# A decoder layer whose feed-forward part gets a written-out order on every engine

## The chip, the cores and the metric

The kernel runs on one core of a Trainium2 chip. The core has five engines that work side by side, each with its own queue of instructions that it takes in order: TensorE (PE: matrix products and transposes; PEld is its loading of the stationary operand), VectorE (DVE), ScalarE (ACT), GpSimd (POOL) and SyncE (SP, which here only issues DMAs). They meet through semaphores. The metric is the time of one execution on the device in microseconds.

## The reference, cut to what matters

One step of a one-layer decoder, for a prompt of 1024 rows and 8 sample rows with the same weights; the model width is 1024, the feed-forward width 22 x 128 = 2816. The change lies behind the mixing of the two attention paths:

```python
mixed = (jax.nn.sigmoid(ga) * y_att + jax.nn.sigmoid(gb) * y_ret) @ w_o
x = _layer_norm(DEEPNORM_ALPHA * x + gate1 * mixed, ln1_g, ln1_b)
h2 = x * (1 + scale2) + shift2
f_gate, f_up = jnp.split(h2 @ w_ffn_in, 2, axis=-1)
ff = (jax.nn.silu(f_gate) * f_up) @ w_ffn_out
x = _layer_norm(DEEPNORM_ALPHA * x + gate2 * ff, ln2_g, ln2_b)
```

gate, scale and shift are vectors computed from c at the start. Beside this the outputs hold the rolled key and value caches of the sample rows, which are copied by DMAs of some 2 MB through the whole kernel.

## The kernel before, in words

**Products.** Each f32 operand is split in two parts: ScalarE casts the raw tile to `hi` (L158), VectorE subtracts to get `lo` (L159). A product is three matmuls: hi x hi, hi x lo, lo x hi (`mm3`, L195 to L197; `product`, L1033 to L1036).

**w_o and the first layer norm.** Four chunks of 256 columns of the transposed activations (the first also has the 8 sample rows). In each, 8 blocks `f` of 24 matmuls; ScalarE evacuates a block into `gm` with the gate (L1084). After the 8 blocks `norm_block` runs for each 128 rows: 8 transposes of gm into `ps_a` (L939), residual and layer norm on VectorE, 8 transposes of x into `ps_b` (L949), and h2. After two chunks `combine_chunk` forms the seven left operands X1 to X7 of a half.

**First matrix of the feed-forward.** A 2 x 2 scheme with seven products. A job is one block of 128 columns of the gate and of the up part. `pair_load` loads the two weight tiles g and u and has GpSimd form four sums of them (L1006 to L1009); `pair_split` splits the four tiles that result (two products each from the first three, one from the last); `pair_steps` runs the seven steps, each of 12 matmuls for one half of the rows, with the evacuations by ScalarE (copies L1044, L1052, L1058; SiLU L1049, L1068) and VectorE (L1048, L1059, L1063, L1064, L1067, L1069) into the tile `c`. The result goes to DRAM (`ffd`, L1070). There are 25 jobs: 3 with half 1 alone, 19 with both halves (168 matmuls each), 3 with half 0 alone. While jobs run, `roll` starts one cache copy per split: VectorE copies one element (`tk`, L171), GpSimd copies it on (`tick`, L172) and issues the DMA (L174).

**Second matrix.** For half 1, then half 0: 8 column blocks `f`, each 22 x 3 matmuls into each of two banks, with the weights in three groups of 8, 8 and 6 row blocks. The activations come back from DRAM (`ffr`, L1110) and are split into `xk`. ScalarE evacuates into `z` (L1221); after every second f, z is transposed for each block of 128 rows (L1236), VectorE adds it to y (L1237) and takes statistics (L1238). GpSimd scales and shifts the residual (L1193). `finish` does the last layer norm: for half 1 on GpSimd (L1160, L1167) with the write of y on SP's queue (L1168), for half 0 on VectorE (L1162, L1172).

**What sets the order.** The program is written as loops, and a scheduler of the language orders the instructions of each engine by its own estimates: an instruction may be put ahead of others that stand before it in the text as long as its data allow. Tiles come from rings (`stream`, by tag) and from a list of free slots; an instruction that writes a tile waits until its former readers are done. On the chip an engine keeps the order that it was given.

## Time and profile before

| | us |
|---|---|
| median of 3 runs | 1992.9 (1992.45 to 1998.88) |
| profiled execution | 1996.48 |
| its span | 1994.7 |
| mean granted TensorE clock in it | 0.965 |
| TensorE busy | 1859.9 (93%) |
| VectorE, ScalarE, GpSimd busy | 966.3, 678.5, 474.5 |

The profile shows one execution. Its stages from w_o on, by the first matmul of each: w_o at 1020.4 us, first single jobs at 1143.9, jobs with both halves from about 1200 to 1640, last single jobs to 1686, second matrix to 1977.2, then the last layer norm and the writes to 1994.7. A clock of 1.00 is the full 2.4 GHz, the lower level is half of that; a mean between them says how much of a stretch ran at which.

### The profile page before, as it was taken

The page shows a single profiled execution, that of the slowest core. Times are in us where ns is not written, and L with a number is a line of the kernel's source. Part 1 is how long each engine was busy: PE and PEld are TensorE (multiplying, and loading weights), DVE is VectorE, ACT ScalarE, POOL GpSimd, SP SyncE. Part 2 cuts the span into 40 slices and gives each one's busy share as a digit, 9 for nine tenths or more (in the row PEclk, how much of TensorE's full clock was granted, in tenths as well). Part 3 has the DMA queues.
Part 4 walks back from the last instruction along what each step waited for, and adds up shares of the span by engine and source line. Part 5 has one row for each costly group of instructions (what it writes and reads, how often), then busy time and mean ns, then how long its engine had stood idle before and what let it go on. Part 6 is the DMA issues. An engine that isn't in the chain of part 4 may idle for free. (4 is left out here: it accounts for less than half of the span.)

```text
span 1994.7 us, 33810 instructions
## 1 busy us (share of the span) xinstructions
PE 1859.9 (93%) x13974; PEld 1760.4 (88%) x13974; DVE 966.3 (48%) x2009; ACT 678.5 (34%) x1327; POOL 474.5 (24%) x492
## 2 busy tenths in 40 slices
PE   7999999999999999999998879999999997899796
PEld 5979798899989999999998778989899887899696
DVE  4644546676443422214549583345444558435324
ACT  3251424343433421223236543333332344224221
POOL 2000010320000000000024445433432446504800
PEclk9999999999999999999999889999999998999898
DMA  9212131852231344512145534344554557435331
GB/s 289 74 36 92 33 110 54 221 178 75 67 102 53 112 146 146 156 54 64 54 148 190 161 129 135 136 149 149 192 204 144 192 169 226 137 97 177 119 93 59
DMA packets 263899, 255.34 MB, mean 128 GB/s; under 512 B 9701, under 2 KB 243533, under 8 KB 262978
## 3 DMA queue, kind: packets, MB, share of 16 engines
q1 hardware_dynamic: 240530, 138.48, 23.9%
q0 software_dynamic: 23088, 114.61, 16.7%
q8 instruction: 109, 1.79, 0.4%
q14 instruction: 44, 0.36, 0.1%
q10 hardware_dynamic: 128, 0.10, 0.0%
HBM read 222.25 MB, written 74.94 MB: 149 GB/s over the span
## 5 line engine op out<-in xcount | busy, mean ns | idle before, releaser
L159 DVE TENSOR_TENSOR w_lo<-w_raw,w_hi 128x1024 fp32r<-128x1024 f32 (+1 forms) x186 | 235.3, 1266 | 398.9 <-ACT w_hi L158 397.3
L158 ACT CAST w_hi<-w_raw 128x1024 fp32r<-128x1024 f32 (+1 forms) x202 | 203.0, 1005 | 433.3 <-PE ps_d L196 223.3
L195 PE MATMUL ps_d<-h_hi,w_hi 128*128 128x384 f32 (+1 forms) x1008 | 325.5, 323 | 0.0
L197 PE MATMUL ps_d<-h_hi,w_lo 128*128 128x384 f32 (+1 forms) x1008 | 323.7, 321 | 0.0
L196 PE MATMUL ps_d<-h_lo,w_hi 128*128 128x384 f32 (+1 forms) x1008 | 323.2, 321 | 0.0
L1216 PE MATMUL ps_d<-xk,w_hi 128*128 128x260 f32 (+1 forms) x704 | 201.2, 286 | 1.2 <-DVE xk L159 1.2
L1215 PE MATMUL ps_d<-xk,w_hi 128*128 128x260 f32 (+1 forms) x704 | 201.5, 286 | 0.0
L1217 PE MATMUL ps_d<-xk,w_lo 128*128 128x260 f32 (+1 forms) x704 | 200.4, 285 | 0.0
L1033 PE MATMUL ps_b<-X,w_hi 128*128 128x260 f32 (+1 forms) x528 | 160.6, 305 | 38.7 <-ACT w_hi L158 29.5
L195 PEld LDWEIGHTS ps_d<-h_hi,w_hi 128*128 128x128 f32 x1008 | 189.5, 188 | 5.2 <-DVE A L846 3.3
L197 PEld LDWEIGHTS ps_d<-h_hi,w_lo 128*128 128x128 f32 x1008 | 189.7, 188 | 1.7 <-issue 1.2
L196 PEld LDWEIGHTS ps_d<-h_lo,w_hi 128*128 128x128 f32 x1008 | 189.7, 188 | 0.8 <-issue 0.4
L1036 PE MATMUL ps_b<-X,w_lo 128*128 128x260 f32 (+1 forms) x528 | 158.9, 306 | 2.7 <-DVE w_lo L159 1.7
L1035 PE MATMUL ps_b<-X,w_hi 128*128 128x260 f32 (+1 forms) x528 | 158.7, 301 | 0.0
L1033 PEld LDWEIGHTS ps_b<-X,w_hi 128*128 128x128 f32 x528 | 109.7, 208 | 43.3 <-ACT w_hi L158 32.5
L1216 PEld LDWEIGHTS ps_d<-xk,w_hi 128*128 128x128 f32 x704 | 134.9, 192 | 1.4 <-DVE xk L159 1.4
L1215 PEld LDWEIGHTS ps_d<-xk,w_hi 128*128 128x128 f32 x704 | 135.0, 192 | 0.1
L1217 PEld LDWEIGHTS ps_d<-xk,w_lo 128*128 128x128 f32 x704 | 135.1, 192 | 0.0
L172 POOL COPY tick<-tk 1x1 f32<-1x1 f32 x54 | 39.6, 734 | 385.3 <-DVE tk L171 374.0
L363 PE MATMUL ps_d<-w_lo,h_hi 128*128 128x256 f32 x448 | 127.3, 285 | 0.7 <-DVE w_lo L159 0.7
L361 PE MATMUL ps_d<-w_hi,h_hi 128*128 128x256 f32 x448 | 127.5, 285 | 0.0
L362 PE MATMUL ps_d<-w_hi,h_lo 128*128 128x256 f32 x448 | 126.7, 283 | 0.0
(358 smaller groups left out, 4605.1 us busy)
## 6 DMA issues: line engine op xcount, KB each, us to landing
w_raw<-w_in SPq DMA_DIRECT2D x56, 512.0 KB, 4.5
w_raw<-w_ffn_in SPq DMA_DIRECT2D x50, 512.0 KB, 4.0
ada_raw<-w_ada SPq DMA_DIRECT2D x32, 512.0 KB, 4.9
w_raw<-w_o SPq DMA_DIRECT2D x32, 512.0 KB, 3.9
w_raw<-w_ffn_out SPq DMA_DIRECT2D x32, 512.0 KB, 3.9
sample_k<-cache_k POOLq DMA_DIRECT2D x8, 2047.0 KB, 9.4
sample_v<-cache_v POOLq DMA_DIRECT2D x8, 2047.0 KB, 9.3
ada_raw<-w_ada SPq DMA_DIRECT2D x32, 256.0 KB, 5.3
```

Source lines behind the costliest of these rows:

```text
L158: nc.scalar.copy(hi, raw)
L159: eng.tensor_sub(lo, raw, hi.bitcast(F32))
L195: nc.tensor.matmul(ps, whi[:, k0 + k, :], xhi[:, t0:t0 + n], start=f, stop=False)
L196: nc.tensor.matmul(ps, whi[:, k0 + k, :], xlo[:, t0:t0 + n], start=False, stop=False)
L197: nc.tensor.matmul(ps, wlo[:, k0 + k, :], xhi[:, t0:t0 + n], start=False, stop=l)
L361: nc.tensor.matmul(ps[:, j, :], xh, whi, start=k == 0, stop=False)
L1033: nc.tensor.matmul(ps, whi[:, w, :], xhi[:, k, :n], start=first and k == 0, stop=False, skip_group_check=True)
L1035: nc.tensor.matmul(ps, whi[:, w, :], xlo[:, k, :n], start=False, stop=False, skip_group_check=True)
L1036: nc.tensor.matmul(ps, wlo[:, w, :], xhi[:, k, :n], start=False, stop=k == 3, skip_group_check=True)
L1215: nc.tensor.matmul(ps, whi[:, kk, :], xt[:, 0, j, :n], start=st_, stop=False)
L1216: nc.tensor.matmul(ps, whi[:, kk, :], xt[:, 1, j, :n], start=False, stop=False)
L1217: nc.tensor.matmul(ps, wlo[:, kk, :], xt[:, 0, j, :n], start=False, stop=en)
```

## The change

Everything up to w_o is as before. From there on TensorE, VectorE, ScalarE, GpSimd and SP are reached through a wrapper, `InOrder`, which pins each traced instruction behind the one that was traced before it on the same engine, so the text's order is the engine's order. A few calls still go past the wrapper (w_o's loads and splits, the layer norm's VectorE work). The text is rewritten to suit:

- `norm_block` is a generator in two parts. The first part of a block (transposes of gm, residual, norm) runs after one of the next chunk's w_o blocks, the second (transposes of x, h2) some blocks later; those of the last chunk run between the products of the first single jobs.
- In a job both halves' products of a step are issued first, then both evacuations. The splits stand at fixed steps: tile 2 and 3 of the running job after steps 0 and 1, tile 0 and 1 of the next job after steps 2 and 4. The four sums of the next job follow step 0, the loads of the one after it step 1. u is loaded into a slot, g into the ring. Cache copies start in the jobs with both halves, four a job instead of three, and in half 1 of the second matrix.
- In the second matrix the weights are loaded four groups ahead and split two ahead. The transposes of a pair of f come after the first group of the next f, the blocks in a row. The activations' loads are on SP's queue, half 1's writes of y on GpSimd's, and the residual's scale and shift on VectorE. The last f of half 0 is done bank by bank, with the norm of two blocks after each.

The core of the diff:

```diff
+class InOrder:
+    def __init__(self, tc, eng):
+        self.tc, self.eng = tc, eng
+
+    def __getattr__(self, op):
+        f = getattr(self.eng, op)
+
+        def call(*args, **kw):
+            return self.tc.keep_in_program_order(f(*args, **kw))
+
+        return call
...
+    def psplit(raw, hi, lo):
+        act.copy(hi, raw)
+        dve.tensor_sub(lo, raw, hi.bitcast(F32))
...
         layer_norm(x, rows)
         dma_o.dma_start(xr[tb:tb + rows], x[:rows])
+        yield
         for half in range(2):
             pb = bbank((128, 4, rows))
             for j in range(4):
                 f = 4 * half + j
-                nc.tensor.transpose(pb[:, j, :], x[:rows, 128 * f:128 * f + 128], ident[:rows, :rows])
+                pe.transpose(pb[:, j, :], x[:rows, 128 * f:128 * f + 128], ident[:rows, :rows])
...
+    def norm_chunk(ci, gm):
+        t0 = QCH[ci][0]
+        todo = [(t0, 128), (t0 + 128, 128)] + ([(S, NB)] if ci == 3 else [])
+        gens = []
+        for tb, rows in todo:
+            dst = h2s
+            if tb < S:
+                dst = H2[tb // 128] = slots.alloc((128, 8, 128), name="h2")
+            g_ = norm_block(tb, rows, gm, t0, dst)
+            next(g_)
+            gens.append(g_)
+            yield
+        slots.free(*gm)
+        if ci == 0:
+            combine_chunk(1)
+            yield
+        for g_ in gens:
+            next(g_)
+            yield
+
...
+    def pair_sums(q):
+        if q >= NJ:
+            return
+        g, _, u, _ = raws[q]
         s_, e = slots.alloc((128, 8, 128), name="w_s"), slots.alloc((128, 4, 128), name="w_s4")
...
-        nc.scalar.copy(c11, pa)
+        yield
+        act.copy(c11, pa)
         yield
         pg = dbank((128, n))
         product(pg, q, 0, 1, x[2], n, True)
-        nc.vector.tensor_add(c11, c11, pg)
-        nc.scalar.activation(c11, c11, AF.Silu)
...
-    JOBS = [(i, (1,)) for i in range(LEAD)] + [(i, (1, 0)) for i in range(LEAD, FFC)] + [(i, (0,)) for i in range(LEAD)]
+    pending = deque()
+
+    def step_pending():
+        while pending:
+            try:
+                next(pending[0])
+                return
+            except StopIteration:
+                pending.popleft()
+
+    def after_chunk(ci, gm):
+        yield from norm_chunk(ci, gm)
+        if ci % 2 == 0:
+            if ci == 2:
+                combine_chunk(3)
+            combine_chunk(ci)
+            yield
...
         for f in range(8):
             ps = dbank((128, n))
             o0 = t0 % 512
-            mm3(ps, wo_cols(f), [(m[ci // 2][:, 0, :], m[ci // 2][:, 1, :]) for m in mix], o0, n)
+            whi, wlo = wo_cols(f)
+            for k, m in enumerate(mix):
+                xhi, xlo = m[ci // 2][:, 0, o0:o0 + n], m[ci // 2][:, 1, o0:o0 + n]
+                pe.matmul(ps, whi[:, k, :], xhi, start=k == 0, stop=False)
+                pe.matmul(ps, whi[:, k, :], xlo, start=False, stop=False)
+                pe.matmul(ps, wlo[:, k, :], xhi, start=False, stop=k == 7)
             dst = gm[f // 2][:, f % 2, :]
             nc.scalar.activation(dst[:, :256], ps[:, :256], AF.Copy, scale=modT[:, GATE1 + f, 8:9])
             if n > 256:
                 nc.vector.tensor_mul(dst[:, 256:n], ps[:, 256:n], modT[:, GATE1 + f, 0:NB])
+            step_pending()
         if ci % 2 == 0:
             slots.free(*[m[ci // 2] for m in mix])
...
-        dma_o.dma_start(raw[:, :, :n], ffd[k, half].rearrange("p (a b) -> p a b", a=2)[:, :, :n])
+        sp.dma_start(raw[:, :, :n], ffd[k, half].rearrange("p (a b) -> p a b", a=2)[:, :, :n])
         t = xk[half][k] = slots.alloc((128, 2, 2, 260), F32R, name="xk")
-        split(raw[:, :, :n], t[:, 0, :, :n], t[:, 1, :, :n])
+        return raw, t, n
...
     for q, (i, halves) in enumerate(JOBS):
...
         steps = [pair_steps(q, i, half) for half in halves]
         for s_ in range(7):
-            for g_ in steps:
-                next(g_)
-            if more and s_ in (1, 3, 5):
-                pair_split(q + 1, s_ // 2)
-            if q >= FFC and 1 <= s_ < 5:
-                ff_load(1, ORDER[4 * (q - FFC) + s_ - 1])
...
+            for _ in range(2):
+                for g_ in steps:
+                    next(g_)
+            if s_ == 0:
+                pair_split(q, 2)
+                pair_sums(q + 1)
+            elif s_ == 1:
+                pair_split(q, 3)
+                pair_load(q + 2)
+            elif s_ == 2:
+                pair_split(q + 1, 0)
+            elif s_ == 4:
+                pair_split(q + 1, 1)
+            if len(halves) == 1 and s_ % 2 == 0 or q > LEAD - 2:
+                step_pending()
...
+            pool.tensor_mul(y[:rows], y[:rows], ln2[0][:rows])
+            pool.tensor_add(y[:rows], y[:rows], ln2[1][:rows])
+            pool.dma_start(dst, y[:rows])
...
+    def residual(e):
+        y, rows = e[0], e[3]
+        dve.scalar_tensor_tensor(y[:rows], y[:rows], ALPHA, ln1[0][:rows], op0=OP.mult, op1=OP.mult)
+        dve.scalar_tensor_tensor(y[:rows], ln1[1][:rows], ALPHA, y[:rows], op0=OP.mult, op1=OP.add)
...
+        out_mm(G, (0, 1))
...
+        if G > 0:
+            out_split(G + 2)
+        out_load(G + 4)
+        if o0 == 0 and later:
+            for e in ents[later[0]]:
+                add_block(e, *later[1:])
+            slots.free(later[2])
+            if later[:2] == (1, 7):
+                late_ys = deque(ents[1])
+            later = None
...
-        finish(*e)
+                later = (half, f, z)
```

In the rows below a number behind a name only tells tiles apart, and in the kernel after all instructions that the wrapper passes have the wrapper's line, L116.

**ScalarE, around the start of a job with both halves.** `c4` are the output tiles of the two halves, `ps_b` a bank of products, `w_s` and `w4` tiles of sums. Before:

```order
L1044 COPY c4_367_12206<-ps_b_12207 128x260
L1044 COPY c4_368_12221<-ps_b_12222 128x256
L1049 ACTIVATE c4_367_12206<-c4_367_12206 128x260
L1049 ACTIVATE c4_368_12221<-c4_368_12221 128x256
L158 CAST w_hi_12131<-w_s_360_12061 128x1024
L158 CAST w_hi_12168<-w_raw_12058 128x1024
L158 CAST w4_hi_363_12192<-w_s4_361_12062 128x512
L158 CAST w_hi_12266<-w_raw_12196 128x1024
L1052 COPY c4_367_12206<-ps_b_12207 128x260
L1052 COPY c4_368_12221<-ps_b_12222 128x256
L1058 COPY c4_367_12206<-ps_b_12207 128x260
L1058 COPY c4_368_12221<-ps_b_12222 128x256
```

and now:

```order
L116 COPY c4_371_12396<-ps_b_12397 128x260
L116 COPY c4_372_12410<-ps_b_12411 128x256
L116 CAST w_hi_12426<-w_raw2_364_12071 128x1024
L116 ACTIVATE c4_371_12396<-c4_371_12396 128x260
L116 ACTIVATE c4_372_12410<-c4_372_12410 128x256
L116 CAST w4_375_12470<-w_s4_368_12192 128x512
L116 COPY c4_371_12396<-ps_b_12397 128x260
L116 COPY c4_372_12410<-ps_b_12411 128x256
L116 CAST w_hi_12507<-w_raw_12234 128x1024
L116 COPY c4_371_12396<-ps_b_12397 128x260
L116 COPY c4_372_12410<-ps_b_12411 128x256
L116 CAST w_hi_12569<-w_s_373_12434 128x1024
```

Before, the job's remaining casts stand in a row behind the SiLUs of its second step; now each cast stands alone between evacuations, and the last one belongs to the next job already.

**TensorE, at the end of the first w_o chunk.** `ps_d_10440` is that chunk's last block, `gm` its evacuated blocks, `mix` the activations. Before:

```order
L196 MATMUL ps_d_10440<-mix_283_10063,w_hi_10443 128x264
L197 MATMUL ps_d_10440<-mix_283_10063,w_lo_10444 128x264
L939 MATMUL ps_a_10476<-ident_72,gm_285_10205 128x128 x2
L939 MATMUL ps_a_10476<-ident_72,gm_286_10206 128x128 x2
L939 MATMUL ps_a_10482<-ident_72,gm_287_10207 128x128 x2
L939 MATMUL ps_a_10482<-ident_72,gm_288_10208 128x128
L195 MATMUL ps_d_10601<-mix_269_9167,w_hi_10604 128x256
L196 MATMUL ps_d_10601<-mix_269_9167,w_hi_10604 128x256
```

and now, where `ps_d_10477` is the next chunk's first block, which follows ps_d_10440:

```order
L116 MATMUL ps_d_10477<-mix_281_9935,w_lo_10481 128x256
L116 MATMUL ps_d_10477<-mix_283_10063,w_hi_10480 128x256 x2
L116 MATMUL ps_d_10477<-mix_283_10063,w_lo_10481 128x256
L116 MATMUL ps_a_10512<-ident_72,gm_285_10205 128x128 x2
L116 MATMUL ps_a_10512<-ident_72,gm_286_10206 128x128 x2
L116 MATMUL ps_a_10518<-ident_72,gm_287_10207 128x128 x2
L116 MATMUL ps_a_10518<-ident_72,gm_288_10208 128x128 x2
L116 MATMUL ps_d_10534<-mix_269_9167,w_hi_10537 128x256 x2
```

Before, the transposes of gm follow the chunk's last block at once; now the next chunk's whole first block is between.

**SP's queue in half 0 of the second matrix.** `w_raw` are the weights' tiles, `y` the finished rows of half 1. Before:

```order
L1208 DMA w_raw_18979<-w_ffn_out 128x8x128
L1208 DMA w_raw_19033<-w_ffn_out 128x8x128
L1168 DMA y_prompt<-y_538_17120 128x1024
L1168 DMA y_prompt<-y_539_17121 128x1024
L1208 DMA w_raw_19087<-w_ffn_out 128x3x128 x2
L1168 DMA y_prompt<-y_540_17122 128x1024
L1168 DMA y_prompt<-y_541_17123 128x1024
L1208 DMA w_raw_19135<-w_ffn_out 128x8x128
L1168 DMA y_sample<-y_542_17124 8x1024
L1208 DMA w_raw_19189<-w_ffn_out 128x8x128
```

and now:

```order
L116 DMA w_raw_18768<-w_ffn_out 128x8x128
L116 DMA w_raw_18838<-w_ffn_out 128x8x128
L116 DMA w_raw_18896<-w_ffn_out 128x3x128 x2
L116 DMA w_raw_18954<-w_ffn_out 128x8x128
L116 DMA w_raw_19013<-w_ffn_out 128x8x128
L116 DMA w_raw_19087<-w_ffn_out 128x3x128 x2
```

The writes of y have left this queue (they stand on GpSimd's); only loads of weights follow each other here.

## Rows read from the trace of the kernel before

**Rows 1.** Windows: per stretch busy time of each engine (x instructions), PEclk, DMA share, GB/s.
```profile
1020.40:1143.90 123.50, 110.13 (x886) 108.08 (x886) 83.42 (x147) 67.36 (x121) 52.06 (x31) 0.96 0.60 189
1143.90:1200.00 56.10, 43.91 (x307) 41.33 (x308) 46.29 (x76) 26.66 (x51) 24.19 (x29) 0.85 0.40 130
1274.44:1298.39 23.95, 21.98 (x170) 21.51 (x169) 9.37 (x19) 7.28 (x14) 10.32 (x12) 0.93 0.38 132
1322.39:1342.34 19.95, 19.95 (x170) 19.95 (x169) 6.38 (x14) 4.88 (x11) 5.79 (x7) 1.00 0.48 159
1640.00:1686.00 46.00, 33.66 (x230) 32.65 (x230) 37.53 (x44) 22.71 (x40) 29.20 (x33) 0.82 0.75 241
1686.00:1977.20 291.20, 266.41 (x2178) 263.74 (x2177) 109.24 (x170) 80.44 (x115) 97.89 (x61) 0.95 0.38 116
1900.00:1950.00 50.00, 50.00 (x423) 49.56 (x422) 15.88 (x25) 11.34 (x15) 0.00 (x0) 1.00 0.32 93
1977.20:1994.70 17.50, 1.56 (x10) 0.82 (x8) 13.73 (x28) 1.43 (x5) 0.00 (x0) 0.68 0.32 120
```

**Rows 2.** Waits of TensorE, 1018 us to the end: us in total, times, longest.
```profile
PE ps_b L1033 <- ACT w_hi L158: 29.5, 15, 2.0
PE ps_a L1236 <- ACT z L1221: 23.6, 5, 14.7
PE ps_a L939 <- ACT gm L1084: 12.2, 5, 4.2
...
PE ps_d L1216 <- DVE xk L159: 1.2, 1, 1.2
```

**Rows 3.** Timeline between two jobs: start, us, engine, operation [idle before].
```profile
1439.19 0.42 ACT L1049 ACTIVATE c<-c 128x256 f32<-128x256 f32 x1 [0.99 <-DVE c L1048]
1439.51 1.03 ACT L158 CAST w_hi<-w_s 128x1024 fp32r<-128x1024 f32 x1
...
1440.45 1.04 ACT L158 CAST w_hi<-w_raw 128x1024 fp32r<-128x1024 f32 x1
...
1440.59 0.48 PE L1033 MATMUL ps_b<-X,w_hi 128*128 128x260 f32 x1 [1.96 <-ACT w_hi L158]
```

**Rows 4.** Groups by line, jobs with both halves: x count, busy, mean ns, idle before.
```profile
L159 DVE TENSOR_TENSOR w_lo<-w_raw,w_hi 128x1024 fp32r<-128x1024 f32 x39 | 51.7, 1326 | 2.3 <-ACT w_hi L158 2.1
...
L172 POOL COPY tick<-tk 1x1 f32<-1x1 f32 x31 | 32.6, 1053 | 88.1 <-DVE tk L171 76.8 <-DVE c L1067 11.2
```

**Rows 5.** Timeline of VectorE and GpSimd in a last single job.
```profile
1642.95 4.95 DVE L159 TENSOR_TENSOR w_lo<-w_raw,w_hi 128x1024 fp32r<-128x1024 f32 x1
1642.99 1.38 POOL L1007 TENSOR_TENSOR w_s<-w_s,w_raw 128x512 f32<-128x512 f32 x1
...
1645.43 1.37 POOL L1009 TENSOR_TENSOR w_s<-w_raw,w_s 128x512 f32<-128x512 f32 x1
```

**Rows 6.** Timeline of ScalarE at a chunk boundary of w_o.
```profile
1076.44 1.04 ACT L158 CAST w_hi<-w_raw 128x1024 fp32r<-128x1024 f32 x1
1077.39 0.47 ACT L1084 ACTIVATE gm<-ps_d,modT 128x256 f32<-128x256 f32 x1
```

**Rows 7.** Timeline in half 0 of the second matrix.
```profile
1868.82 4.64 POOL L1167 TENSOR_TENSOR y<-y,ln_b 128x1024 f32<-128x1024 f32 x2
1871.18 2.65 SPq L1168 DMA_DIRECT2D y_prompt<-y  x2
...
1877.91 0.83 ACT L158 CAST w_hi<-w_raw 128x768 fp32r<-128x768 f32 x1 [16.41 <-DMA w_raw<-w_ffn_out]
```

**Rows 8.** Timeline of VectorE behind transposes of half 1.
```profile
1726.71 0.41 DVE L1237 TENSOR_TENSOR y<-y,ps_a 128x256 f32<-128x256 f32 x1
...
1727.98 0.42 DVE L1238 BATCH_NORM_STATS2 bny<-y 128x6 f32<-128x256 f32 x1
```

**Rows 9.** Timeline of VectorE in the tail.
```profile
1980.92 1.28 DVE L1162 SCALAR_TENSOR_TENSOR y<-y,bnmv,ln_g 128x1024 f32<-128x1024 f32 x1
...
1983.44 2.73 DVE L1172 SCALAR_TENSOR_TENSOR y<-y,bnr,ln_b 128x512 f32<-128x512 f32 x4
```

More of the change, by code (lines that the diff above doesn't have):

```diff
@@ L1113, in ff_load, with out_load @@
         slots.free(raw)
-    rolling[0] = True
+    GROUPS = [(half, f, o0, nk) for half in (1, 0) for f in range(8) for o0, nk in ((0, 8), (8, 8), (16, 6))]
+    NG = len(GROUPS)
+    graw, gw = {}, {}
+    def out_load(G):
+        if G >= NG:
+            return
+        _, f, o0, nk = GROUPS[G]
+        raw = graw[G] = stream.tile([128, nk, 128], F32, tag="raw", name="w_raw")
+        ks = ORDER[o0:o0 + nk]
+        k1 = next((j for j in range(1, nk) if ks[j] != ks[j - 1] + 1), nk)
+        for j0, j1 in ((0, k1), (k1, nk)):
+            if j1 > j0:
+                sp.dma_start(raw[:, j0:j1, :], w_fo[128 * ks[j0]:128 * (ks[j0] + j1 - j0), 128 * f:128 * f + 128]
+                             .rearrange("(k p) c -> p k c", p=128))
@@ L1116, in tile_hybrid_decoder_step, with out_split @@
+    def out_split(G):
+        if G >= NG:
+            return
+        nk = GROUPS[G][3]
+        hi = stream.tile([128, nk, 128], F32R, tag="hi", name="w_hi")
+        lo = stream.tile([128, nk, 128], F32R, tag="lo", name="w_lo")
+        psplit(graw.pop(G)[:], hi[:], lo[:])
+        if rolling[0]:
+            roll(hi)
+        gw[G] = (hi, lo)
+    waiting = deque()
+    kq = 0
     for q, (i, halves) in enumerate(JOBS):
-        more = q + 1 < len(JOBS)
+        rolling[0] = len(halves) == 2
@@ L1136, in tile_hybrid_decoder_step, with bcast @@
+    assert not pending
     free_x(X[0])
[L1137 to L1140 removed]
+    def bcast(names):
         ts = []
@@ new lines, in add_block @@
+    def add_block(e, f, z):
+        y, st, tb, rows, _, _ = e
+        c = slice(128 * (f - 1), 128 * f + 128)
+        pz = abank((rows, 256))
+        for p in range(2):
+            if tb < S:
+                b = tb // 128 % 4
+                src = z[:, p, b % 2, 128 * (b // 2):128 * (b // 2) + 128]
+            else:
+                src = zs[:, f - 1 + p, :]
+            pe.transpose(pz[:, 128 * p:128 * p + 128], src, ident[:])
+        dve.tensor_add(y[:rows, c], y[:rows, c], pz)
+        dve.bn_stats(st[:rows, f // 2, :], y[:rows, c])
@@ new lines, in tile_hybrid_decoder_step, with out_mm @@
+    zs = late.tile([128, 8, NB], F32, name="zs")
+    ln1, ln2 = bcast(("ln1_g", "ln1_b")), bcast(("ln2_g", "ln2_b"))
+    ents = {1: list(load_ys(1))}
+    todo = deque(ents[1])
+    later = None
+    late_ys = deque()
+    pss = None
+    rolling[0] = True
+    def out_mm(G, js):
+        half, f, o0, nk = GROUPS[G]
+        n = HALF[half]
+        whi, wlo = gw[G]
+        for j in js:
+            for kk in range(nk):
+                xt = xk[half][ORDER[o0 + kk]]
+                pe.matmul(pss[j], whi[:, kk, :], xt[:, 0, j, :n], start=o0 + kk == 0, stop=False)
+                pe.matmul(pss[j], whi[:, kk, :], xt[:, 1, j, :n], start=False, stop=False)
+                pe.matmul(pss[j], wlo[:, kk, :], xt[:, 0, j, :n], start=False, stop=o0 + kk == FFC - 1)
@@ new lines, in evac, with refill, drain @@
+    def evac(half, f, z, j):
+        act.activation(z[:, f % 2, j, :256], pss[j][:, :256], AF.Copy, scale=modT[:, GATE2 + f, 8:9])
+        if half:
+            dve.tensor_mul(zs[:, f, 4 * j:4 * j + 4], pss[j][:, 256:260], modT[:, GATE2 + f, 4 * j:4 * j + 4])
+    def refill(half, room):
+        k = len(xk[half])
+        if k < FFC and len(slots.free_list) >= room:
+            waiting.append(ff_load(half, ORDER[k]))
+            return True
+    def drain():
+        while waiting:
+            ff_split(waiting.popleft())
@@ new lines, in tile_hybrid_decoder_step @@
+        out_mm(G, (0, 1))
+        if half and f == 7:
+            for k in ORDER[o0:o0 + nk]:
+                slots.free(xk[1][k])
+        rolling[0] = bool(half)
+        if G > 0:
[7 more added lines that the diff above has]
+                late_ys = deque(ents[1])
+            later = None
+        if o0 == 16:
+            for j in range(2):
+                evac(half, f, z, j)
+            if f % 2:
+                later = (half, f, z)
@@ new lines, in tile_hybrid_decoder_step @@
+        if half and f == 6 and o0 == 16:
+            while refill(0, 5):
+                pass
+            drain()
+        if half and f == 7:
+            for _ in range(nk):
+                refill(0, 5)
+                if len(waiting) > 2:
+                    ff_split(waiting.popleft())
+            drain()
+        if not half and f == 0:
+            while refill(0, 2):
+                pass
+            drain()
+            if o0 == 16:
+                ents[0] = list(load_ys(0))
+                todo = deque(ents[0])
@@ L1250 @@
+        if todo and o0 < 16:
+            residual(todo.popleft())
+            if todo:
+                residual(todo.popleft())
+        if late_ys and o0 == 8:
+            finish(*late_ys.popleft())
+    assert not copies, len(copies)
 OUTPUTS = ([("y_prompt", (S, D)), ("y_sample", (NB, D))]
```

253 lines of the change are left out of this document (111 added, 142 removed).

## The prediction

> **What bounds the kernel now.** I read the windows by stage first, then what TensorE waited for, then the timeline at those waits. All rows are from the stretch that the change touches, 1020 us to the end; nothing ahead of it is edited, so I cost that part at nothing.
>
> The windows give the price of a matmul at the full clock: 423 instructions in 50 us with no idle time, 118 ns each [rows 1]. With it each stage's own work is worked out from its count in the window, and the rest of the stage is loss: w_o 886 x 0.118 = 104.5 of 123.5 us, 19.0 lost; the first single jobs 307 x 0.118 = 36.2 of 56.1, 19.9 lost; the last single jobs 230 x 0.118 = 27.1 of 46.0, 18.9 lost; the second matrix 2184 (2112 matmuls and 72 transposes by the loops) x 0.118 = 257.7 of 291.2, 33.5 lost; the tail 17.5 with TensorE nearly still [rows 1].
>
> For the 19 jobs with both halves, compare two of them: one takes 23.95 us at a clock of 0.93, another 19.95 us at 1.00 [rows 1]. 19.95 is 168 x 0.118 = 19.8, so the second loses nothing. The list of waits shows why the other is longer: TensorE waits for w_hi 15 times, 29.5 us in all, longest 2.0 [rows 2]; the four others of the 19 don't. So a stalled job loses 2.0 us of waiting and another 2.0 to matmuls that run at the lower of the two clocks behind it (the mean of 0.93 against 1.00) and to small waits for w_lo. The timeline of one shows the mechanism: on ScalarE the SiLU of the second half (1439.19) ends, only then the cast of w_hi starts (1439.51), and TensorE, idle for 1.96 us, starts in 1440.59 [rows 3]. The cast needed nothing that was late; its data were loaded and summed. It stood behind the SiLU, which stood behind VectorE's addition, which stood behind the last matmul of the second product. 15 x 4.0 = 60 us is the largest sum that the profile offers.
>
> **The change, part by part.** *Jobs with both halves.* The order of ScalarE now puts each cast ahead of the SiLU or behind a copy, at least one step ahead of need. A step is 24 matmuls, 24 x 0.118 = 2.83 us. Step 0's copies end about 0.4 us after it, at 3.2; the cast for steps 4 and 5 takes 1.04 [rows 3], to 4.3; VectorE's w_lo 1.33 [rows 4], to 5.6; needed at 4 x 2.83 = 11.3. The next job's first cast follows step 2's copies, 8.9, done with its w_lo at 11.3, needed at 19.8; its second follows step 4's copies, 14.5, done at 16.9, needed at 25.5. The slack is 5.7 us or more each time. What can use it up is GpSimd: its four sums follow step 0 too, and they hold VectorE up. One w_lo took 4.95 us while three sums of 1.37 to 1.38 ran [rows 5], 3.6 more than the mean of 1.33. With all four ahead of it, 4 x 1.37 = 5.5, w_lo ends at 11.1 against 11.3: just in time. Ends for this part: all 60 us gone, or the present loss kept (0). I take 55, since the middle case is in time by rows and a few jobs will miss.
>
> The Trainium skill (SBUF — State Buffer, Who interferes with whom) states that a VectorE instruction with two SBUF inputs and a GpSimd instruction that reads SBUF exclude each other, and that the one that issues first keeps the port for its whole instruction. By that alone w_lo would wait for one sum; here it outlasted three, so the trace is harsher than the rule read instruction by instruction. By the rule this part would give 60; by the row it gives the rival with a kept wait, below.
>
> *w_o and the layer norms.* Before, the transposes of gm stand right behind the last block of a chunk, whose evacuation has to come first; TensorE waits for gm 5 times, 12.2 us, longest 4.2 [rows 2]. Now a whole block of 24 matmuls (2.83 us) lies between. But the evacuation still stands on ScalarE behind a cast of the next w_o block: 1.04 and 0.47 [rows 6], and that cast needs a buffer which the running block lets go. So I expect 1.5 to 2 us to stay at each of three chunk boundaries, and the clock to fall there again. Between 0 and 15 of the 19.0; I take 6, half of the waiting on gm.
>
> *First single jobs.* The last chunk's norms, the combinations and their splits now come between the products. VectorE is busy 46.3 of 56.1 us there [rows 1] and loses none of this work, so at best 9.8 come back; and with a pinned order an instruction of VectorE that waits for a transpose holds up the w_lo behind it. From 4 lost to 9.8 gained: I take 2 gained.
>
> *Last single jobs.* VectorE 37.5 of 46.0 us, clock 0.82 [rows 1]: at best 8.5 come back, by loading and splitting the activations of the second matrix one at a time between steps. Here a late ffr holds up ScalarE's queue, as nothing may pass it. Ends 5 lost and 8.5 gained; I take 5 gained.
>
> *Second matrix.* Of its 33.5 us, 23.6 are waits of the transposes for z [rows 2]. The longest, 14.7: ScalarE stood 16.41 us in a cast that waited for its w_raw [rows 7]; the load stood on SP's queue behind the writes of y_prompt, and those behind GpSimd's normalisation of y, 2.3 us an instruction (4.64 for two) [rows 7]. Now SP holds loads alone there, the writes are on GpSimd's queue, where only GpSimd waits for them, and the residual left GpSimd for VectorE, which has room (15.9 of 50 us [rows 1]). Putting the transposes off by one group, 48 matmuls or 5.7 us, takes z out of their way. All 33.5 would be the upper end. What comes in: five blocks (half 1) or four (half 0) of transposes in a row on two banks, so that from the third on each waits for VectorE's addition and statistics, 0.41 + 0.42 [rows 8], less the 0.2 to 0.4 that its own transposes and the start take: about 0.45 a time, 4 sets x 3 x 0.45 + 3 sets x 2 x 0.45 = 8.1. At the start the last activations come late, since they are written out and read back first: the start now waits 1.2 for one of them [rows 2], with nothing put off; I take 3.5, an estimate, between 1.2 and 6. At the change of halves 20 loads of ffr and their casts stand ahead of z on ScalarE: the four shorter waits for z make 23.6 - 14.7 = 8.9 now, a third to nearly all of that may stay; I take 6. 33.5 - 8.1 - 3.5 - 6 = 16 gained. The lower end is 5 lost, should the stall at the change of halves stay as it is now.
>
> *Tail.* In the 17.5 us two pairs of blocks follow each other on VectorE: the first pair's normalisation from 1980.9 to 1986.2, the last four instructions of it 2.73 [rows 9], then the second pair's. Now the last f is done bank by bank, and the first pair's lies beside 66 matmuls (7.8 us). About 5.3 go, 0.9 comes back as a wait ahead of the last 66, and the write at the end stays: 4 gained, between 2 and 6.
>
> Sum: 55 + 6 + 2 + 5 + 16 + 4 = 88. Against the profiled execution, 1996.5 - 88 = 1908.5; that execution is 3.6 us above the median of the runs shown (1992.9), so I state 1905. The bounds of the sum: all lower ends together 0 + 0 - 4 - 5 - 5 + 2, 12 lost; all upper ends 60 + 15 + 9.8 + 8.5 + 33.5 + 6 = 133 gained, 1860.
>
> **Rivals.** *A wait stays in the jobs with both halves.* With all four sums ahead, w_lo was in time by 0.2 us; ticks and DMA issues between the sums (a tick 1.05 on average [rows 4]) push them later. If w_lo is late by 1.5 us in each of 19 jobs and the clock falls behind it as today (the same again, less the part that is already late: 1.0), 19 x 2.5 = 47 of the 60 stay lost; 60 - 47 = 13 instead of 55, so 1905 + 42 = 1947. For it: the row of 4.95. Against it: VectorE has 10 us to spare in a job (9.37 and 6.38 busy [rows 1]), and the collision needs the sums exactly there.
>
> *Nearly all comes back.* If the pinned order meets no late data, the losses go but for VectorE's work in the first singles and the transposes: 60 + 10 + 5 + 8 + 24 + 5 = 112, 1881; at the very best 1860. For it: only 15.9 of 50 us VectorE in the second matrix. Against it: VectorE's share in the single jobs.
>
> *Slower than before.* One mechanism: products wait for their evacuations. In the new code a step issues the products of both halves and only then their copies; the next product but one adds into the same bank and may not start ahead of the copy. If on ScalarE a cast that waits for data or for a buffer stands ahead of that copy, TensorE waits in every step. The other parts give 33, so it decides from the point where the 19 jobs together take 439 (15 x 23.95 + 4 x 19.95) + 33 = 472 us, 24.8 each: 0.7 us lost per step. At 1.0 us a step these jobs take 133 more and 60 less than now: 1992.9 - 33 + 73 = 2033. For it: 15 of 19 jobs show what one cast ahead of its turn costs. Against it: between the copy and the product that needs it lies a step of 2.83 us, and by the order each cast's buffer was last read a step or more before.
>
> **How the numbers follow.** Forecast (1905, own range 1884 to 1930): 0.58. A wait stays (1930 to 1965): 0.20. Nearly all (1860 to 1884): 0.08. Slower: 0.09. What is left, 0.05, is a gain eaten up to within 0.3% (6 us, about what a measurement can tell from no change). Range 1868 to 1955: it leaves out the slower case, the top of the kept wait and the best end, 0.18 in all. Faster 0.86, same 0.05, slower 0.09.
>
> **What would show it.** In the profile after: TensorE's waits for w_hi between two jobs gone, jobs of 20.0 us at a clock of 1.00; waits for w_lo of no more than 5 us over all 19. gm with about 5 us. In the second matrix no wait of 14 us, but rows of 0.4 to 0.5 us of transposes for VectorE's y, and ScalarE waiting for ffr at the change of halves. The tail 13 us. I am wrong if TensorE waits for w_lo or for copies in most jobs, or if the singles become longer.

## The result, and the profile after

The changed kernel takes 1928.3 us (median of 4 runs, 1925.95 to 1931.58) against 1995.9 us for the kernel before in the same comparison (1992.45 to 2000.09): a ratio of 0.9662, 95% interval 0.9634 to 0.969. It is faster, by 68 us; 1905 was forecast. In three of the runs told of below (e3, e8, e10) one or two executions were disturbed, among them the profiled ones of e3 and e8, so their medians leave these out and no stage of e3 and e8 is read.

The windows by stage of the profiled execution after (stretch, length, busy time of PE, PEld, DVE, ACT and POOL, each with its count, PEclk, DMA share, GB/s), to be read beside [rows 1]:

```profile
1019.80:1131.74 111.94, 106.03 (x881) 104.88 (x880) 80.67 (x143) 66.57 (x121) 48.06 (x31) 0.98 0.70 216
1131.74:1192.30 60.56, 42.77 (x285) 40.82 (x286) 53.09 (x72) 29.70 (x51) 23.96 (x18) 0.83 0.29 90
1192.30:1573.10 380.80, 380.80 (x3193) 380.80 (x3193) 195.37 (x343) 136.25 (x266) 157.68 (x189) 1.00 0.57 189
1573.10:1614.10 41.00, 32.83 (x254) 31.62 (x253) 32.30 (x44) 22.32 (x40) 20.21 (x21) 0.96 0.75 241
1614.10:1640.00 25.90, 21.07 (x152) 19.84 (x151) 17.81 (x21) 10.14 (x16) 0.69 (x1) 0.94 0.64 202
1640.00:1760.00 120.00, 115.49 (x950) 113.08 (x949) 49.30 (x83) 32.35 (x46) 0.00 (x0) 1.00 0.40 118
1760.00:1775.00 15.00, 10.57 (x72) 9.63 (x71) 13.22 (x29) 10.04 (x16) 0.00 (x0) 0.89 0.62 184
1775.00:1797.00 22.00, 22.00 (x189) 22.00 (x188) 11.76 (x17) 11.48 (x15) 19.60 (x12) 1.00 0.63 210
1797.00:1820.00 23.00, 13.51 (x79) 12.83 (x79) 22.66 (x18) 2.24 (x3) 13.04 (x8) 0.72 0.36 110
1820.00:1911.40 91.40, 89.67 (x751) 88.49 (x749) 28.68 (x43) 18.86 (x27) 0.00 (x0) 0.99 0.23 70
1911.40:1924.20 12.80, 0.81 (x6) 0.34 (x4) 8.45 (x16) 1.06 (x3) 0.00 (x0) 0.70 0.33 123
```

The third line is the gain: 19 jobs in 380.8 us, TensorE busy in all of it at a clock of 1.00. The second and the ninth are the losses. By stage, with the kernel before cut at the same events (the first matmul of each stage):

| stage | before | after | change | forecast |
|---|---|---|---|---|
| w_o | 123.8 | 111.9 | -11.9 | -6 |
| first single jobs | 52.5 | 60.6 | +8.1 | -2 |
| 19 jobs with both halves | 440.6 | 380.8 | -59.8 | -55 |
| last single jobs | 48.8 | 41.0 | -7.8 | -5 |
| second matrix | 291.2 | 297.3 | +6.1 | -16 |
| tail | 17.5 | 12.8 | -4.7 | -4 |

The list of TensorE's waits from 1010 us on, in us in total, times, longest, answers to [rows 2]:

```profile
PE ps_d L116 <- DVE w_lo L116: 9.8, 3, 6.7
PE ps_a L116 <- DVE y L116: 8.0, 18, 2.4
PE ps_b L116 <- ACT c L116: 7.4, 6, 2.8
PE ps_b L116 <- DVE w_lo L116: 6.7, 1, 6.7
PE ps_b L116 <- DVE h L977: 6.3, 2, 4.6
PE ps_a L116 <- DVE c L116: 5.3, 4, 2.2
PE ps_d L116 <- DVE zs L116: 5.0, 2, 3.4
...
PE ps_b L116 <- ACT w_hi L116: 1.5, 1, 1.5
```

The 29.5 us for w_hi and the 23.6 us for z are gone but for 2.1 and 0.9. What stands there now is mostly VectorE, 42 of 57 us; the longest are two waits of 6.7 us for w_lo, one at the first single job, one in half 0. The timeline around the second shows who held it up (start, us, engine, operation; the rows of VectorE, GpSimd and the late matmul):

```profile
1797.97 2.39 POOL L116 TENSOR_TENSOR y<-y,ln_g 128x1024 f32<-128x1024 f32 x1
1798.19 3.25 DVE L116 SCALAR_TENSOR_TENSOR y<-ln_b,y 128x1024 f32<-128x1024 f32 x1
1800.43 3.20 POOL L116 TENSOR_TENSOR y<-y,ln_b 128x1024 f32<-128x1024 f32 x1
1801.36 3.36 DVE L116 TENSOR_TENSOR w_lo<-w_raw,w_hi 128x1024 fp32r<-128x1024 f32 x1
...
1804.77 0.58 PE L116 MATMUL ps_d<-xk,w_lo 128*128 128x256 f32 x1 [6.72 <-DVE w_lo L116]
```

VectorE's residual (the stage's new work) and w_lo alternate with GpSimd's norm of half 1. A w_lo of 3.36 us stands beside a mean of 1.33 in [rows 4]; the stretch from 1797 to 1820 does 79 x 0.118 = 9.3 us of TensorE's work in 23 us.

### The profile page after: what moved, and what is told of

It reads as the page before. It is cut to its first block, busy times and chain, and to the rows that moved or that the text cites. A ratio compares the mean times of both kernels' runs of the same rounds, so it can differ in the third digit from the quotient of the medians.

```text
span 1924.2 us, 33797 instructions
## 1 busy us (share of the span) xinstructions
PE 1832.1 (95%) x13974; PEld 1737.1 (90%) x13974; DVE 983.0 (51%) x2027; ACT 679.1 (35%) x1329; POOL 376.3 (20%) x433
## 4 chain that ended last, share of the span: by engine, by line
PE 74%; issue 12%; DVE 6%; DMA 4%; ACT 2%; SPq 1%; POOL 1%; DVEq 0%; ACTq 0%; POOLq 0%
PE ps_d L116 15%; PE ps_d L208 10%; PE ps_b L116 9%; PE ps_d L209 9%; PE ps_d L210 9%; PE ps_a L116 6%; PE ps_d L376 2%; PE ps_d L375 2%; PE ps_d L374 2%; PE ps_a L490 1%; DVE y L116 1%; PE ps_b L508 1%; PE ps_o L517 1%; DVE w_lo L116 1%; PE ps_a L241 1%
## 5 line engine op out<-in xcount | busy, mean ns | idle before, releaser
L116 PE MATMUL ps_d<-xk,w_hi 128*128 128x260 f32 (+1 forms) x1408 | 260.0, 287 | 6.8 <-DVE zs L116 5.0
L172 DVE TENSOR_TENSOR w_lo<-w_raw,w_hi 128x1024 fp32r<-128x1024 f32 x88 | 103.7, 1178 | 256.8 <-ACT w_hi L171 256.1
L116 PEld LDWEIGHTS ps_d<-xk,w_hi 128*128 128x128 f32 x1408 | 221.9, 193 | 8.1 <-DVE zs L116 5.4
L116 DVE TENSOR_TENSOR w_lo<-w_raw,w_hi 128x1024 fp32r<-128x1024 f32 (+1 forms) x98 | 132.3, 1350 | 175.2 <-ACT w_hi L116 175.1
L116 PE MATMUL ps_d<-xk,w_lo 128*128 128x260 f32 (+1 forms) x704 | 201.8, 287 | 9.8 <-DVE w_lo L116 9.8
L116 PE MATMUL ps_b<-X,w_hi 128*128 128x256 f32 (+1 forms) x1056 | 195.6, 285 | 10.5 <-ACT c L116 7.4
L171 ACT CAST w_hi<-w_raw 128x1024 fp32r<-128x1024 f32 x104 | 103.9, 999 | 256.6 <-PE ps_d L209 203.1
L116 PEld LDWEIGHTS ps_b<-X,w_hi 128*128 128x128 f32 x1056 | 164.9, 191 | 12.2 <-ACT c L116 8.6
L116 PE MATMUL ps_b<-X,w_lo 128*128 128x260 f32 (+1 forms) x528 | 150.3, 285 | 6.7 <-DVE w_lo L116 6.7
L116 ACT CAST w_hi<-w_raw 128x1024 fp32r<-128x1024 f32 (+1 forms) x98 | 99.3, 1014 | 143.6 <-PE ps_d L116 142.1
L116 PEld LDWEIGHTS ps_d<-xk,w_lo 128*128 128x128 f32 x704 | 136.2, 193 | 10.4 <-DVE w_lo L116 10.4
L116 PE MATMUL ps_d<-X,w_hi 128*128 128x256 f32 (+1 forms) x704 | 130.9, 286 | 0.0
L116 PEld LDWEIGHTS ps_d<-X,w_hi 128*128 128x128 f32 x704 | 110.5, 192 | 0.0
```

The lines of the kernel that those rows point to most:

```text
L116: return self.tc.keep_in_program_order(f(*args, **kw))
L171: nc.scalar.copy(hi, raw)
L172: eng.tensor_sub(lo, raw, hi.bitcast(F32))
```

## The experiments

All are against the kernel before; a stage's length is read from the profiled execution. Stages of the changed kernel to compare with: w_o 111.9, first single jobs 60.6, half 1 of the second matrix 144.5, half 0 152.8. The part ahead of w_o, which no edit touches, ends between 1017.6 and 1024.9 us in these profiles, and the intervals of e2, e4 and e5 overlap the changed kernel's. So what these three edits do is read from stages, and from e10, which joins them.

**e1, one cast late.**

```diff
-            elif s_ == 2:
-                pair_split(q + 1, 0)
             elif s_ == 4:
                 pair_split(q + 1, 1)
+            elif s_ == 6:
+                pair_split(q + 1, 0)
```

> The changed kernel with one edit: the cast and split of the next job's first weight tile (q+1, 0) stand behind the last step of the running job instead of behind step 2, so on ScalarE this cast follows the last SiLU again. Theory (the gain in the jobs with both halves comes from where that cast stands): TensorE waits about 2 us for w_hi or its w_lo at the start of each of the 19 jobs and runs on the low clock behind it, a job takes 24 us instead of 20.04, the whole about 70 us longer, near 1998 us. Rival (the gain comes from issuing both halves' products before the evacuations, or from the pinned order as such): a job stays under 21 us and the whole under 1950 us.

Measured: 2051.9 us (one run). The jobs with both halves take 484.2 us, 25.5 each. Their window, and the waits of the whole stretch from w_o on:

```profile
1205.10:1689.30 484.20, 426.45 (x3192) 418.06 (x3192) 188.45 (x342) 136.84 (x266) 152.26 (x191) 0.90 0.44 149
```
```profile
PE ps_b L116 <- ACT w_hi L116: 52.7, 25, 3.6
PE ps_b L116 <- DVE w_lo L116: 31.3, 16, 6.2
```

The place of this one cast decides the stage: behind the last SiLU it costs more than the whole gain, with everything else of the change in place. The size expected, 4 us a job, was too small: it is 5.4. In each of the 19 jobs TensorE waits 1.9 to 2.3 us for w_hi and then 0.6 to 2.4 for the w_lo behind it (58 us in all; in five of the jobs a GpSimd sum beside it stretches that w_lo to 2.9 us); the other 45 go with matmuls at the lower clock, 0.90 on the mean. The rest of the 25 and 16 waits listed are in the single jobs.

**e9, the new text without pins.**

```diff
-            return self.tc.keep_in_program_order(f(*args, **kw))
+            return f(*args, **kw)
```

> The changed kernel with one edit: the wrapper passes every call on without pinning it, so the text is the new one and the scheduler orders it by its own estimates. Theory (the pins keep the casts where the text has them, and that is where the 58 us in the jobs with both halves come from): the scheduler puts some casts behind SiLUs again, a job takes 21 to 24 us on average, and the whole lies between 1945 and 1990 us. Rival (the new text alone does it, by issuing both halves' products first and splitting earlier): jobs of 20.0 to 20.5 us, whole at 1935 us or less, where free floating may even mend the change of halves.

Measured: 1946.9 us, ratio 0.9745 (0.9708 to 0.9783). Windows of the first single jobs, the jobs with both halves and half 1 in its profile, and the wait for w_hi from 1200 to 1570 us:

```profile
1142.50:1189.20 46.70, 38.83 (x287) 37.05 (x286) 45.37 (x69) 30.45 (x52) 18.16 (x16) 0.92 0.34 106
1189.20:1611.30 422.10, 399.71 (x3193) 395.22 (x3192) 195.42 (x350) 142.77 (x271) 168.80 (x192) 0.96 0.53 177
1657.90:1790.00 132.10, 130.68 (x1088) 129.91 (x1087) 58.73 (x97) 39.96 (x58) 0.72 (x2) 1.00 0.44 130
```
```profile
PE ps_b L116 <- ACT w_hi L116: 17.6, 9, 2.0
```

The theory holds for the jobs with both halves: w_hi is waited for 9 times again, 2.0 us each, and the pins are worth 422 - 381 = 41 us there. The new text alone gives the other 19 of the 60. Elsewhere the pins cost: without them the first single jobs are 14 us shorter, with VectorE busy in 45.4 of 46.7 us, and half 1 is 12 us shorter; w_o is 6.7 us and the last single jobs 5 us longer.

**e2, half 1's norm on VectorE.**

```diff
-            pool.tensor_mul(y[:rows], y[:rows], ln2[0][:rows])
-            pool.tensor_add(y[:rows], y[:rows], ln2[1][:rows])
+            dve.tensor_mul(y[:rows], y[:rows], ln2[0][:rows])
+            dve.tensor_add(y[:rows], y[:rows], ln2[1][:rows])
```

> The changed kernel with one edit: the last layer norm of half 1 multiplies and adds ln2 on VectorE instead of GpSimd. Theory (at the change of halves VectorE's residual and w_lo, two operands from SBUF each, alternate with GpSimd's ten instructions of the same kind, so each takes 3.3 us instead of 1.2): the residual's instructions take 1.2 to 1.3 us, the wait of 6.7 us for w_lo and the low clock behind it go, second matrix 297 to about 284 us, whole near 1915 us. Rival (VectorE simply has too much to do there, 22.7 of 23 us busy, and the rows of y come late): ten more instructions of 1.2 us on VectorE keep the wait or lengthen it, second matrix 297 us or more, whole 1928 us or more.

Measured: 1921.7 us, ratio 0.9626 (0.9597 to 0.9656). Half 0 takes 147.4 us. The same stretch of half 0, and one instruction of the residual:

```profile
1797.00:1820.00 23.00, 17.90 (x133) 17.26 (x132) 13.93 (x20) 5.73 (x7) 1.06 (x2) 0.85 0.36 110
```
```profile
1799.88 1.22 DVE L116 SCALAR_TENSOR_TENSOR y<-ln_b,y 128x1024 f32<-128x1024 f32 x1
```

These 23 us hold only three of the ten instructions that moved, so the busy time in them, 13.9 for 22.7 us, isn't that of the same work. All ten lie between 1775 and 1820 us; that stretch in the changed kernel and in e2:

```profile
1775.00:1820.00 45.00, 35.51 (x266) 34.83 (x265) 34.42 (x34) 13.72 (x18) 32.64 (x19) 0.86 0.49 159
1775.00:1820.00 45.00, 39.90 (x320) 39.26 (x319) 32.92 (x45) 14.68 (x19) 4.79 (x9) 0.92 0.53 171
```

VectorE does 45 instructions instead of 34 and is busy no longer, since each of this size takes 1.22 us and not 3.3. So it was GpSimd's neighbourhood, not the amount of work. The wait of 6.7 us is gone; another, 4.0 us for y, takes part of its place, so 7 us came of the 13 expected.

**e5, mean and root of the last norm pinned.** A pin ties an instruction to the one traced just before it on its engine. In the last norm (`finish`) that one is a reciprocal which isn't pinned, so the scheduler moved it forward, and the pinned instruction behind it with it. On VectorE, of the norms written one per f (`nb`), the second to the fourth stand together ahead of the next w_lo of the first f:

```
L116 TENSOR_TENSOR w_lo_18711<-w_raw_18554,w_hi_18710 128x1024
L116 TENSOR_SCALAR nb_18722<-bnmv_18717,bnr_18718 128x1
L116 TENSOR_SCALAR nb_18908<-bnmv_18903,bnr_18904 128x1
...
L116 TENSOR_SCALAR nb_19095<-bnmv_19090,bnr_19091 128x1
...
L116 TENSOR_SCALAR nb_19261<-bnmv_19256,bnr_19257 128x1
L116 TENSOR_TENSOR w_lo_18765<-w_raw_18635,w_hi_18764 128x1024
```

The edit:

```diff
-        mv, r = ln_aggr(st[:, 0:parts, :], rows)
+        dve.bn_aggr(mv[:rows], st[:rows, 0:parts, :].rearrange("p a b -> p (a b)"))
+        act.activation(r[:rows], mv[:rows, 1:2], AF.Sqrt, bias=eps[:rows, 0:1], scale=1.0)
+        dve.reciprocal(r[:rows], r[:rows])
```

> The changed kernel with one edit: in the last layer norm the three instructions for mean and root (aggregate, square root, reciprocal) are pinned too. In the changed kernel they are not, and as a pin only ties an instruction to the one traced just before it on its engine, the scheduler pulled the norms of five blocks, written one per f, up together into the first two f of half 0. Theory (that pile of ten GpSimd instructions is what VectorE's residual and w_lo alternate with): with one norm per f most residual instructions take 1.2 us, the wait of 6.7 us for w_lo goes, half 0 falls from 152.8 to about 143 us, whole near 1918 us. Rival (the wait comes from late rows of y and too much VectorE work at that place): half 0 stays at 150 us or more, whole 1926 us or more.

Measured: 1921.9 us, ratio 0.964 (0.960 to 0.9679); half 0 144.2 us, about as expected (143), the whole 4 us above. GpSimd's norms are apart, and the residual between them runs undisturbed. Half 0, then two neighbours on GpSimd, then an instruction of the residual:

```profile
1763.70:1907.90 144.20, 132.96 (x1096) 130.17 (x1095) 69.87 (x105) 43.96 (x62) 33.24 (x19) 0.99 0.38 116
```
```profile
1788.17 2.10 POOL L116 DMA_DIRECT2D y<-xr  x4
1807.13 2.37 POOL L116 TENSOR_TENSOR y<-y,ln_g 128x1024 f32<-128x1024 f32 x1 [16.85 <-ACT y L116]
```
```profile
1794.02 1.23 DVE L116 SCALAR_TENSOR_TENSOR y<-y,ln_g 128x1024 f32<-128x1024 f32 x1 [5.46 <-DMA y<-xr]
```

**e4, transposes two blocks at a time.** The blocks wait in a queue, and the loop takes two of them after each run of 24 matmuls:

```diff
-        out_mm(G, (0, 1))
+        out_mm(G, (0,))
+        spread(2)
+        out_mm(G, (1,))
...
-            for e in ents[later[0]]:
-                add_block(e, *later[1:])
+            spread(2)
```

> The changed kernel with one edit: the put-off transposes of the second matrix stand two blocks at a time between runs of 24 matmuls, instead of all four or five blocks in a row. Theory (from the third block on each waits for VectorE, as only two banks are there): the 18 waits for y, 8.0 us, fall to a few, under 2.5 us, the second matrix 297 to about 291 us, whole near 1922 us. Rival (VectorE takes the additions late anyhow, behind w_lo): the waits stay near 8 us, whole 1928 us.

Measured: 1919.5 us, ratio 0.9611 (0.9568 to 0.9653). The waits for y fall from 18 to 2:

```profile
PE ps_a L116 <- DVE y L116: 1.9, 2, 1.6
```

Half 1 is 5 us shorter, half 0 nearly 7: 12 us in the second matrix, twice the 6 expected. Of TensorE's waits not only 6.1 us for y are gone but also that of 3.4 us for zs at the change of halves; the one for w_lo there stays (7.0 us).

**e3 and e6, the combinations pinned.** In `combine` the splits and differences of the left operands, which go past the wrapper in the changed kernel, go through the pinned engines, in e3 for both halves, in e6 for half 0 alone.

```diff
-            split(v, X[p][0][:, :, c], X[p][1][:, :, c])
+            psplit(v, X[p][0][:, :, c], X[p][1][:, :, c])
...
-        nc.vector.tensor_sub(x11, x12, x11)
+        dve.tensor_sub(x11, x12, x11)
```

> The changed kernel with one edit: the combinations and splits of the left operands (combine) also go through the pinned engines; in the changed kernel they don't, and the scheduler put four of VectorE's ahead of the w_lo of the first product. Theory (those instructions, stretched to 1.7 us by GpSimd's sums, are why TensorE waits 6.7 us at the first job): that wait falls to under 3 us and the first single jobs take 54 to 56 us instead of 60.6, whole near 1923 us. Rival (VectorE bounds this stage with 53 of 60.6 us, so the work only comes later): another wait takes its place, the stage stays at 59 to 62 us, whole 1928 us.

> The changed kernel with one edit: only the combinations of half 0 are pinned to their place between the products of the first single jobs; those of half 1 stay free as in the changed kernel. Theory (four floated VectorE instructions ahead of the first w_lo cost 6.7 us, and what made the version with all combinations pinned slower was the half 1 part, now late): the wait at the first job falls under 3 us and the first single jobs take 54 to 57 us instead of 60.5, whole near 1923 us. Rival (VectorE bounds the stage, whatever comes first): the wait reappears later, the stage stays at 59 us or more, whole 1928 us or more.

Measured: e3 1934.5 us, ratio 0.9695 (0.9664 to 0.9727); e6 1932.9 us, ratio 0.9689 (0.9647 to 0.9732). Neither is shorter than the changed kernel, and e6's first single jobs take 63.4 us. In e6 the wait at the first job falls from 6.7 to 1.1 us, and others come in its place:

```profile
PE ps_a L116 <- DVE c L116: 9.3, 4, 5.7
...
PE ps_a L116 <- DVE x L960: 5.2, 1, 5.2
...
PE ps_b L116 <- DVE w_lo L116: 1.1, 1, 1.1
```
```profile
1134.20:1197.60 63.40, 42.67 (x284) 40.63 (x285) 46.77 (x73) 30.77 (x54) 22.10 (x18) 0.84 0.27 84
```

Both theories miss. The four floated instructions explained one wait and not the stage. The rival's figures came (another wait, a stage of 59 us or more), but not for its reason: VectorE doesn't bound the stage, it is busy in 46.8 of 63.4 us. It stands idle in its fixed order, which e9 bears out: left free, most of the same work (69 instructions for 73) fills 45.4 of 46.7 us.

**e7, the evacuation ahead of the splits at the change of halves.**

```diff
-                if len(waiting) > 2:
-                    ff_split(waiting.popleft())
-            drain()
+                if len(waiting) > 4:
+                    ff_split(waiting.popleft())
+            if o0 == 16:
+                drain()
```

> The changed kernel with one edit: at the change of halves the splits of the reloaded activations stand up to four loads behind their loads and after the evacuation of the last f of half 1, instead of ahead of it. Theory (the evacuation stands on ScalarE and VectorE behind splits that wait for loads): the wait of 3.4 us for zs goes and the first groups of half 0 start without a gap, half 0 falls by 3 to 5 us, whole near 1924 us. Rival (half 0's first products need those splits at once, so the wait only moves from zs to xk): no change within 2 us, whole 1928 us.

Measured: 1926.4 us, ratio 0.9668 (0.9628 to 0.9707), no difference from the changed kernel. Half 0 is 1.3 us shorter, half 1 1.8 longer; one wait for zs is left (3.1 us) and the waits for y grow to 12.6. The wait moved, as the rival had it, but to y and not to xk.

**e8, the kernel before with half 1's writes of y on GpSimd's queue.**

```diff
-            dma_w.dma_start(dst, y[:rows])
+            dma_o.dma_start(dst, y[:rows])
```

> The kernel before with one edit: half 1's writes of y are issued on GpSimd's queue instead of SP's. Theory (in the kernel before SP's writes, waiting for GpSimd's norm, held up the weight loads behind them, and so z): the wait of 14.7 us for z goes with its low clock, half 0 falls from 149 to about 133 us, whole about 16 us shorter than before, near 1979 us. Rival (GpSimd's own chain of residual and norm is late for VectorE's additions of half 0 in any case): another wait of 8 us or more takes its place, whole 1988 us or more.

Measured: 1982.5 us, ratio 0.9945 (0.9916 to 0.9974): 11 us, between 5 and 17, where the theory had 16 and the rival at most 7. That the writes held up the loads is borne out in part. Which wait is left couldn't be seen.

**e10 to e12, towards a faster version.** e10 joins e2, e4 and e5; e11 also loads half 0's rows of y two groups earlier; e12 is e10 with pins off in the first single jobs and in half 1:

```diff
-            if o0 == 16:
+            if o0 == 0:
                 ents[0] = list(load_ys(0))
...
-            return self.tc.keep_in_program_order(f(*args, **kw))
+            ins = f(*args, **kw)
+            return self.tc.keep_in_program_order(ins) if InOrder.on else ins
```

> The changed kernel with the edits of e2, e4 and e5 together: norm of half 1 multiplied and added on VectorE, its mean and root pinned, transposes two blocks at a time. Theory (three separate losses: GpSimd against VectorE, norms in a pile, transposes waiting for banks): half 1 139 us as in e4, half 0 from 152.8 to 136 to 140 us, whole 1907 to 1912 us. Rival (the edits mend the same waits at the change of halves, so that their gains don't add): half 0 stays at 143 us or more, whole 1916 us or more.

> The kernel of e10 with one more edit: the rows of y for half 0 are loaded one f-group round earlier (behind the first group of half 0 instead of the third), so they no longer stand on GpSimd's queue behind the first write of half 1's rows. Theory (in e2 the last wait of 4.0 us for y came from residuals that waited for these loads): that wait goes, 2 to 4 us less than e10, whole 1904 to 1908 us. Rival (the loads then compete with those of the activations at the change of halves): no change within 2 us of e10, or a longer wait for xk there.

> The kernel of e10 with pins only in w_o, in the jobs with both halves, in the last single jobs and in half 0; the first single jobs and half 1 of the second matrix are left to the scheduler. Theory (the pins pay where a steady pattern is planned and cost where VectorE or loads bound, as e9 showed: 46.7 against 60.5 us in the first single jobs, 132.1 against 144.4 in half 1, but 422 against 380 in the jobs with both halves): w_o 112, first singles 47 to 50, jobs with both halves 380, last singles 42, half 1 132 to 136, half 0 137 to 142, whole 1886 to 1898 us. Rival (what e9 gained there was work that a stage took over from its neighbour, such as splits done in the stretched jobs before): the first singles or half 1 stay within 4 us of e10's, whole 1904 us or more.

Measured: e10 1907.8 us, ratio 0.9558 (0.953 to 0.9585), an interval clear of the changed kernel's. The three gains nearly add: alone they were 6.7, 8.8 and 6.5 us, 22 together, and e10 has 20.6. In half 0 they share some: 5.4, 6.8 and 8.6 us alone, 16.2 in e10. e11 1914.2 us, ratio 0.9593 (0.9566 to 0.9619), a miss for theory and rival: half 0 takes 145.2 us, with a new wait of 4.5 us for z at the change of halves. e12 1903.5 us, ratio 0.9549 (0.9533 to 0.9566), the lowest time, though its interval and e10's overlap and the 1886 to 1898 expected are missed. Half 0 of e10, then the first single jobs and half 1 of e12:

```profile
1755.50:1892.10 136.60, 131.49 (x1096) 130.24 (x1095) 75.52 (x114) 43.14 (x61) 4.78 (x9) 0.99 0.40 121
1138.20:1186.30 48.10, 38.53 (x287) 36.97 (x286) 46.34 (x71) 29.01 (x51) 17.33 (x15) 0.89 0.37 112
1614.20:1750.20 136.00, 133.50 (x1099) 133.15 (x1099) 64.09 (x101) 40.13 (x57) 0.69 (x1) 0.98 0.44 128
```

The first single jobs are 10 us shorter than in e10 and half 1 5 us, but w_o is 5 and the last single jobs about 6 longer. So some 11 of these 15 us were indeed work that a free stage hands to its neighbour. The 4 left are the difference of e10 and e12, which the overlap of their intervals leaves open.

## Why the prediction was right, and where it was not

The direction, the main term and its mechanism were right; the sum was 88 and the profiled executions differ by 70.5 (1994.7 - 1924.2). The other 6 us of the distance to 1905 are that the profiled execution of before lies 3.6 us above the median that was taken off, and that of after 2.4 below its own. That the sum missed by no more is in part luck: four stages gave 14 us more than forecast, which offset some of the 32 us that two gave less.

- *Jobs with both halves*: 59.8 for 55. The slack worked out from the step of 2.83 us covers GpSimd's sums: w_lo is stretched there (mean 1.49 us for 1.33), and TensorE never waits. The rival with a kept wait did not come. e1 and e9 show that it is the place of the cast; the pins that hold it there are worth 41 us, and the new text gives the other 19 without them.
- *w_o*: 11.9 for 6. Of the evacuation behind a cast, held to cost 1.5 to 2 us three times, one wait of 0.7 us is left; why so little, no run shows.
- *Last single jobs and tail*: 7.8 for 5 and 4.7 for 4. No run takes these two apart.
- *Second matrix*: +6.1 for -16, the step that failed. The stall of 14.7 us went as described. Its sentence "the residual left GpSimd for VectorE, which has room" judged room by busy time alone: the work that came to VectorE reads two operands from SBUF, and so does GpSimd's norm of half 1, which stayed. The row of 4.95 us [rows 5] was weighed for the jobs with both halves and not here. The change of halves costs 6.5 (1760 to 1775) + 13.7 (1797 to 1820) = 20.2 us where 6 was taken. The start costs 8.0 (1614 to 1640) and a wait of 1.6 for zs where 3.5 was; only 1.1 of it are waits for late activations, as the prediction had it, and the longest, 2.6, is for a w_lo behind four instructions of the residual. The transposes' waits came to 8.0, as taken, but e4 shows 12 us to be had from their place. e2 and e5 settle the cause of the larger part, 13.7: without GpSimd's norm half 0 is 5.4 us shorter, with its norms one per f 8.6, and the wait of 6.7 is gone in both.
- *First single jobs*: +8.1 for -2, beyond the end given (4 lost); "if the singles become longer" was one of the prediction's own signs of being wrong, and for these it came. VectorE's busy time rises from 45.2 (the stage cut as in the table) to 53.1 us, as GpSimd's sums fall beside the combinations and w_lo, and it idles in the fixed order besides. The w_lo of the first job is held up (6.7 us), though not by an instruction that waits for a transpose, as that step had it, but by unpinned instructions of the combinations beside GpSimd's sums; taking that wait away (e6) doesn't shorten the stage. Which pin costs the rest is open; e9 and e12 show only that the pins do, and that without them w_o takes back 5 to 7 of the 10 to 14 us.

Of the sentence on SBUF's port: in half 0 VectorE and GpSimd take turns, each waiting for one instruction of the other (3.25 = 1.22 + about 2, beside a GpSimd instruction of 2.4). That is as the Trainium skill has it (SBUF — State Buffer, Who interferes with whom). The row in which one w_lo outlasted three sums didn't recur in the jobs with both halves (the longest w_lo there took 2.16 us).

## What to carry to other kernels

Where an engine waits in a repeating pattern, look at what the late instruction stood behind in its queue; the stage where that one instruction was moved a step ahead gave 60 of this change's 70 us. A written-out order pays in a steady pattern with slack; where one engine is nearly full it can leave that engine idle: there the scheduler's order made the stage 10 to 14 us shorter, though the stage before it gave back half. Before work is moved to an engine "with room", ask what runs on its neighbour at that time, and check in the order that came out that the pins hold what the text says: one unpinned instruction carries its pinned follower along.

## What the runs showed of the hardware

Alternating with GpSimd, VectorE's 128x1024 instructions with two operands from SBUF take 3.25 to 3.4 us instead of 1.2 (w_lo, residual), and of GpSimd's every second 3.2 instead of 2.4. With GpSimd's ten moved to VectorE (e2), VectorE is busy no longer: 32.9 us for 45 instructions, where it was 34.4 for 34. One cast behind its turn cost more in the pinned order (25.5 us a job in e1) than in the order before (23.95 for a stalled job).
